# Where four sums of gate and up weights are made: two moved to DMAs that add in SBUF, two to VectorE, none left on GpSimd

## The chip, the cores and the metric

The kernel runs on one core of a Trainium2 chip. TensorE multiplies matrices (PE in the profile; PEld is its load of weights), VectorE (DVE) and ScalarE (ACT) work on elements, GpSimd (POOL) does so more slowly, SyncE (SP) issues DMAs, and 16 DMA engines move data between HBM and SBUF, the memory on the chip. TensorE writes into eight banks of PSUM. The metric is the device time of one execution in microseconds (us); lower is better.

## The reference

Two layers of a model on 512 tokens of width 1024, in float32. A layer has four stages: a gated feed-forward (FFN), a token mixer of three kinds (attention, mLSTM, RWKV), a second FFN, and a per-layer embedding. The change touches the FFN alone, which runs four times:

```python
x = x + 0.5 * rms_norm(swiglu(rms_norm(x, ln_ffn1_pre[l]), w_ffn1_in[l], w_ffn1_out[l]), ln_ffn1_post[l])
# swiglu(h, w_in, w_out): gate, up = halves of h @ w_in (2816 features each);
#                         (silu(gate) * up) @ w_out
```

`w_ffn1_in` is 1024 x 5632: for each of the 2816 features a gate column and an up column.

## The kernel before

Full float32 precision is had by splitting each operand into a high and a low part and adding three products (`mm3`, L160 to L164: high by high, high by low, low by high). `split` (L139 to L141) makes the parts: ScalarE copies the high part (L140), then VectorE, or GpSimd where it is named, subtracts it from the source for the low part (L141). `wsplit` does this for a 128x512 piece of weights, into one of six buffers of the tag "w" (`NW` = 6).

The features go in 22 tiles of 128. A tile m has four 128x512 pieces of weights: g1 and g2 (the gate columns for the first and the second half of the 1024 inputs) and u1 and u2 (the up columns). With the tokens also in two halves, the plain computation would be eight products of pieces by inputs; Winograd's form needs seven, at the price of sums. `turn` (L204 on) makes the sums of the inputs (t1 to t4, lines L233 to L237) for the tokens' second half, and `unit(m, ...)` in `ffn` makes four sums of the weights on GpSimd (L353 to L356): s1 = u1 + u2, s2 = s1 - g1, s3 = g1 - u1, s4 = g2 - s2. The seven products of a tile are, in the order of the program: 1 (g1) and 2 (g2) in `p1` and `p2`, then in `unit` 6 (s2), 7 (s3), 5 (s1), 3 (s4) and 4 (u2), of 12 matmuls each. Between them VectorE combines the results: L362 (after product 6), L365, L367, L369, L370, L373 and last L376, the product of gate and up into the tile h.

What sets the order: there is no order written out by hand in this loop. The program is written unit after unit, and a planner lays the instructions out on each engine's queue by simulated times, in the order of the program where several are ready; on the chip each queue then runs strictly in order, and an instruction whose data are late holds up all that stand behind it. The planner also gives out the buffers. Those that matter here:

- The weights of a tile (`wr`, 128x2048) go into a slot loaded by two DMAs of 512 KB that SyncE issues (`ffn_load`, L311): the first brings g1 and g2, the second u1 and u2. The first four tiles' slots are loaded ahead of the FFN in `ffn_begin`, whose first splits (product 1 of the four tiles) go to GpSimd; for the tiles after them there are three or four slots, so that the load for tile m waits until an earlier tile has had its last split (product 4).
- The sums (`ws`) take the two buffers of the tag "raw", both for one unit: s1 and s2 in one, s3 and s4 in the other.
- The tag "sg" has two buffers, used outside the loop for the scratch of the norms (`junk`, L191) and, in the stage after it (`ffn_out`), for sums of h.
- In PSUM a bank holds the results of two products. Product 3 goes into the other half of product 6's bank, so it waits until L362 has read product 6.

GpSimd also computes the norms' factors (`rms`, L180 and L181) and, at the start of an FFN, one sum and three low parts of the inputs (L237 and L141 on POOL).

Of the kernel before, what the change touches and what calls it, by code (L numbers as in the profile page):

```python
# [21 lines left out]
EPS = 1e-6  # L22
# [51 lines left out]
class Trunk:  # L74
# [50 lines left out]
    def lanes(self, main=MAINL, aux=AUXL, chain=""):  # L125
        """The PSUM tags that the two kinds of tiles go through in turn."""
        self.main, self.aux = cycle(main), cycle(aux)
        self.chain = chain
# [19 lines left out]
    def wblock(self, ap, name, slot=False, raw=None, eng=None):  # L148
        """A block of weights as two halves, each with its high and low parts."""
        c = ap.shape[1]  # L150
        if raw is None:
            raw = self.wraw.tile([128, c], F32, tag="raw", name=name + "_r")
        self.nc.sync.dma_start(out=raw, in_=ap)
        if slot:
            w = self.slot("h", [2, c], name, F32R)
            self.split(w[:, 0], w[:, 1], raw, eng)
            return [(w[:, 0, i * c // 2:(i + 1) * c // 2], w[:, 1, i * c // 2:(i + 1) * c // 2]) for i in range(2)]
        return [self.wsplit(raw[:, i * c // 2:(i + 1) * c // 2], name, eng) for i in range(2)]
# [17 lines left out]
    def rms(self, ss, scale=1.0):  # L176
        """scale / sqrt(mean + EPS) from two halves of the mean square, each over scale squared."""
        g_ = self.nc.gpsimd
        v, r = self.small("v"), self.small("r")
        g_.tensor_scalar(v, ss[0], ss[1], EPS / (scale * scale), op0=ALU.add, op1=ALU.add)  # L180
        g_.tensor_tensor(r, v, self.mhalf, ALU.pow)  # L181
        return r

    def ssq(self, src, name, scale=1.0, dve=False):
        """A half's part of the mean square, over scale squared."""
        junk = self.tmp.tile([128, 512], F32, tag="sg", name="junk")
        s = self.small(name)
        if dve:
            self.nc.vector.tensor_tensor_reduce(junk, src, src, 1.0 / (D * scale * scale), 0.0, ALU.mult, ALU.add, s)
            return s  # L190
        self.nc.scalar.activation(junk, src, AF.Square, scale=D ** -0.5 / scale, accum_out=s)  # L191
        return s
# [12 lines left out]
    def turn(self, t, xn, ffn):  # L205
# [22 lines left out]
        # the sums of Winograd's form of the product by blocks  # L228
# [5 lines left out]
        v_.tensor_tensor(t1, ps[0], t1, ALU.subtract)  # L234
        v_.tensor_tensor(t2, ps[1], t1, ALU.subtract)
        v_.tensor_tensor(t3, ps[1], t3, ALU.subtract)
        g_.tensor_tensor(t4, t4, t2, ALU.subtract)  # L237
# [19 lines left out]
    def out_proj(self, nb, part, blocks, gain, scale, after, tail):  # L257
        """Token-major product of the feature-major parts with weight blocks, post norm, residual."""
# [48 lines left out]
    def ffn_load(self, l, w, ms):  # L307
        rs = [self.slot("h" if m == 3 else "q", [2, 1024], "wr") for m in ms]
        for i in range(2):
            for m, r in zip(ms, rs):  # L310
                self.nc.sync.dma_start(out=r[:, i], in_=self.ins[f"w_ffn{w}_in"][l, m, i])  # L311
        return rs

# [5 lines left out]
    def ffn(self, l, w, after):  # L319
        """The first product goes by Winograd's form of Strassen's seven products: gate and up features by halves of  # L320
        the inputs, halves of the inputs by halves of the tokens."""
# [27 lines left out]
        def unit(m, r, pa, a):  # L349
            g1, g2, u1, u2 = r[:, 0, 0:512], r[:, 0, 512:1024], r[:, 1, 0:512], r[:, 1, 512:1024]  # L350
            ss = [self.wraw.tile([128, 1024], F32, tag="raw", name="ws") for _ in range(2)]
            s1, s2, s3, s4 = (q[:, i * 512:(i + 1) * 512] for q in ss for i in range(2))
            g_.tensor_tensor(s1, u1, u2, ALU.add)  # L353
            g_.tensor_tensor(s2, s1, g1, ALU.subtract)  # L354
            g_.tensor_tensor(s3, g1, u1, ALU.subtract)  # L355
            g_.tensor_tensor(s4, g2, s2, ALU.subtract)  # L356
            pc, pb, pd = self.aux_tile("p63"), self.aux_tile("p75"), self.mm_tile("p4")
            b = self.tmp.tile([128, S], F32, tag="tb1", name="up", bufs=2)
            # an even tile has the tokens' second half first
# [13 lines left out]
            v_.tensor_tensor(b[:, P], pd[:, L], b[:, P], ALU.add)  # L373
            if m % 4 == 0:
                hs.append(self.slot("h", [8, 256], "h"))
            v_.tensor_tensor(hs[m // 4][:, m % 4 * 2:m % 4 * 2 + 2], a.rearrange("p (i t) -> p i t", i=2),  # L376
                             b.rearrange("p (i t) -> p i t", i=2), ALU.mult)
# [10 lines left out]
        for m in range(NM):  # L388
# [4 lines left out]
            unit(m, *q)  # L393
# [3 lines left out]
    def ffn_out(self, hs, blocks, gain, scale, after):  # L397
        """Token-major product of the features with the output weights, by halves of the model's columns. Some of the
        pairs of feature tiles go by Winograd's form of Strassen's products: halves of the tokens by the tiles of the
        pair by halves of the columns."""  # L400
# [5 lines left out]
        # where the halves of a pair's tiles lie, so that the three that products take as they are lie together  # L406
# [149 lines left out]
    def fm_proj(self, ap, name, halves=False):  # L556
        """Feature-major projection of one 128-column tile."""
# [8 lines left out]
    def tm_proj(self, aps, cols, name, eng=None):  # L566
        """Token-major projection; aps hold the rows in k order. Tokens share a bank where they fit."""
# [83 lines left out]
    def weave(self, l):  # L651
        """The chains of the three mixers, their pieces in the order of the plan; a chain that writes its output over
        the projections' inputs lets the last projection go first."""
# [47 lines left out]
    def rwkv_prep(self, l):  # L701
        """RWKV-7 heads in chunks of 64 tokens. A unit is a chunk c of a pair p of heads; its removal-key and key
        rows are stacked on the partitions, the removal-key rows on half (c + p) % 2."""
# [22 lines left out]
        for p in range(2):  # L726
# [9 lines left out]
            # decay and in-context rate  # L736
# [9 lines left out]
            # normalised removal key  # L746
# [18 lines left out]
            # k (1 + (a - 1) k_a)  # L765
# [6 lines left out]
            # bonus  # L772
# [8 lines left out]
    def rwkv_scores(self):  # L781
# [5 lines left out]
        # token-major keys and values; the values are centered over each head, which centers the outputs  # L787
# [18 lines left out]
        # masked scores of [keys, queries] and the part of the solve's right side that values give  # L806
# [33 lines left out]
        # the removal queries token-major  # L840
# [11 lines left out]
    def rwkv_solve(self, q):  # L852
        """The merged inverse for four chunks, applied to the values' part and to the removal queries, which it
        replaces. Yields between tiles."""
# [6 lines left out]
        # a half of a bank's partitions belongs to one half of the rows  # L861
# [17 lines left out]
    def rwkv_scan(self):  # L879
        """The recurrence over the chunks."""  # L880
# [15 lines left out]
        for c in range(8):  # L896
            st, ns = sts[c % 2], sts[(c + 1) % 2]
            tk = slice(c * 64, (c + 1) * 64)
            if c < 7:
                # the diagonal blocks of the pairs' states  # L900
# [45 lines left out]
    def rwkv_norm(self, yt, eng):  # L946
        """Group norm of the centered heads."""
# [13 lines left out]
    def rwkv_back(self, yt, j):  # L961
        """The way back to feature-major, bonus and output gate."""
# [15 lines left out]
    def invert_blocks(self, sm, z, w):  # L978
        """The blocks of 16 of z = (I - M^T)^-1, for the strictly triangular blocks of 64 whose M^T are in sm."""
# [22 lines left out]
    def invert_merge(self, q, sm, z, w):  # L1002
        """Blocks of 16 merged into blocks of 64, for eight units."""
# [31 lines left out]
    def mlstm_proj(self, l):  # L1035
# [4 lines left out]
        # queries and keys through the causal convolution  # L1040
# [27 lines left out]
        # values, gates  # L1068
# [19 lines left out]
        # running maximum  # L1088
# [38 lines left out]
    def mlstm(self, l):  # L1127
        """The chunks of mLSTM, 128 tokens each."""
# [161 lines left out]
    def attention(self, l):  # L1290
# [10 lines left out]
        # high and low parts: the queries' on the halves of the partitions, the keys' on both  # L1301
# [26 lines left out]
        def softmax(t, g):  # L1328
            # the keys of this tile and the last one, the even tile's first
# [188 lines left out]
```

## Time and profile before

| | |
|---|---|
| time, median of 3 runs | 2371.92 us (2371.49 to 2373.13) |
| profiled execution, span from the first to the last instruction | 2369.3 us (the page gives no other time of it) |
| mean granted TensorE clock | 0.977 of full speed |
| busy: TensorE, VectorE, GpSimd, ScalarE | 90%, 85%, 51%, 49% of the span |
| DMA | 208.78 MB, mean 88 GB/s, all issued by SyncE |

In the profile's rows, "ws<-wr" names output and input tiles without their numbers, "128x512" is partitions by elements, "x88" a count; the numbers after the bar are the busy time in all and the mean of one in ns, and after a second bar stands how long the engine was idle just before and what ended that. L140 and L141 are lines of the helper `split`, so one line stands for many places; the tile's name tells them apart ("w<-wr" is a split of g1, g2 or u2, "w<-ws" one of a sum). In rows in order of time the first number is the start and the second the duration, both in us; VectorE's durations overlap a little with the next start, so costs are read from start to start.

### The profile page before, as it was taken

Reading aid. Unit: us, or ns where it says so; the run is one execution under the profiler, and the core shown is the slowest. Engines: PE = TensorE matmul, PEld = TensorE weight load, DVE = VectorE, ACT = ScalarE, POOL = GpSimd, SP = SyncE. Lnnn points to the kernel's source line nnn. Section 1 sums busy time; section 2 is a strip of 40 time slices with the busy share of each in tenths; the row PEclk is TensorE's granted clock in tenths of the full one; section 3 lists DMA queues with packets and bytes.
Section 4 is the critical chain, followed back from the end, with each engine's and each line's share of the span. In section 5 each row is a group of like instructions: output and inputs, shape, how many; then the busy total and the mean of one; then the engine's idle time right before and its main releaser. Section 6 shows DMA issues by size and latency. Waiting matters only on the chain. (4 is left out here: it accounts for less than half of the span.)

```text
span 2369.3 us, 42540 instructions
## 1 busy us (share of the span) xinstructions
PE 2142.1 (90%) x16592; PEld 1975.2 (83%) x16592; DVE 2019.5 (85%) x2990; ACT 1159.0 (49%) x2262; POOL 1215.5 (51%) x1088
## 2 busy tenths in 40 slices
PE   5899988999998899988989989889999989989898
PEld 5888887988778888887878888888887789889787
DVE  8999999645768999998689999986557699999984
ACT  4444544546545444545554445444474454445443
POOL 5665476132236665566365655751332466555751
PEclk8999999999999999999999999999999999999999
DMA  3222222422031222123411221233220312222232
GB/s 151 90 89 90 71 90 90 147 81 55 20 142 54 86 93 90 63 90 116 134 71 72 92 105 55 84 120 122 68 63 7 143 72 90 90 90 75 78 107 80
DMA packets 67513, 208.78 MB, mean 88 GB/s; under 512 B 15728, under 2 KB 16752, under 8 KB 67312
## 3 DMA queue, kind: packets, MB, share of 16 engines
q1 hardware_dynamic: 67312, 206.07, 25.2%
q8 instruction: 130, 2.13, 0.4%
q14 instruction: 71, 0.58, 0.1%
HBM read 199.23 MB, written 6.82 MB: 87 GB/s over the span
## 5 line engine op out<-in xcount | busy, mean ns | idle before, releaser
L162 PE MATMUL p<-xh,w 128*128 128x256 f32 x1408 | 407.8, 291 | 79.8 <-DVE gate L362 77.5
L164 PE MATMUL p<-xh,w 128*128 128x256 f32 x1408 | 401.6, 286 | 13.6 <-DVE w L141 13.6
L163 PE MATMUL p<-xl,w 128*128 128x256 f32 x1408 | 400.8, 285 | 0.1
L141 DVE TENSOR_TENSOR w<-wr,w 128x512 fp32r<-128x512 f32 x249 | 374.8, 1528 | 10.0 <-ACT w L140 9.8
L140 ACT ACTIVATE w<-ws 128x512 fp32r<-128x512 f32 x352 | 210.6, 623 | 305.0 <-POOL ws L354 178.2
L162 PEld LDWEIGHTS p<-xh,w 128*128 128x128 f32 x1408 | 269.9, 192 | 95.5 <-DVE gate L362 89.7
L141 DVE TENSOR_TENSOR w<-ws,w 128x512 fp32r<-128x512 f32 x352 | 327.7, 935 | 3.2 <-ACT w L140 3.1
L162 PE MATMUL p<-tx,w 128*128 128x256 f32 x1056 | 299.9, 285 | 19.1 <-ACT tx L140 14.7
L164 PE MATMUL p<-tx,w 128*128 128x256 f32 x1056 | 298.9, 284 | 5.3 <-DVE w L141 5.2
L163 PE MATMUL p<-tx,w 128*128 128x256 f32 x1056 | 299.2, 284 | 4.7 <-DVE tx L141 4.7
L164 PEld LDWEIGHTS p<-xh,w 128*128 128x128 f32 x1408 | 270.9, 192 | 14.8 <-DVE w L141 14.8
L353 POOL TENSOR_TENSOR ws<-wr 128x512 f32<-128x512 f32 x88 | 119.0, 1352 | 316.2 <-issue 299.5
L163 PEld LDWEIGHTS p<-xl,w 128*128 128x128 f32 x1408 | 270.8, 192 | 0.7 <-DVE xl L141 0.7
L162 PEld LDWEIGHTS p<-tx,w 128*128 128x128 f32 x1056 | 204.7, 194 | 21.2 <-ACT tx L140 15.3
L164 PEld LDWEIGHTS p<-tx,w 128*128 128x128 f32 x1056 | 203.3, 193 | 7.4 <-DVE w L141 7.1
L163 PEld LDWEIGHTS p<-tx,w 128*128 128x128 f32 x1056 | 203.7, 193 | 5.6 <-DVE tx L141 5.6
L466 PE MATMUL y<-wo,hq 128*128 128x256 f32 x1536 | 189.4, 282 | 3.2 <-DVE up L373 2.7
L140 ACT ACTIVATE w<-wr 128x512 fp32r<-128x512 f32 x264 | 163.3, 625 | 57.7 <-PE p L164 41.9
L466 PEld LDWEIGHTS y<-wo,hq 128*128 128x128 f32 x1536 | 184.5, 189 | 4.8 <-DVE up L373 3.5
L355 POOL TENSOR_TENSOR ws<-wr 128x512 f32<-128x512 f32 x88 | 145.9, 1658 | 46.7 <-DVE w L141 45.0
L354 POOL TENSOR_TENSOR ws<-ws,wr 128x512 f32<-128x512 f32 x88 | 147.4, 1675 | 0.6
L356 POOL TENSOR_TENSOR ws<-wr,ws 128x512 f32<-128x512 f32 x88 | 142.4, 1618 | 5.6
(436 smaller groups left out, 5613.4 us busy)
## 6 DMA issues: line engine op xcount, KB each, us to landing
wr<-in_w_ffn_in SPq DMA_DIRECT2D x176, 512.0 KB, 4.1
ws_r<-in_w_ffn_out SPq DMA_DIRECT2D x56, 512.0 KB, 3.2
wo_r<-in_w_ffn_out SPq DMA_DIRECT2D x32, 512.0 KB, 3.3
pkrv_r<-in_w_rw SPq DMA_DIRECT2D x16, 512.0 KB, 3.5
wpg_r<-in_w_ple_gate SPq DMA_DIRECT2D x16, 512.0 KB, 3.4
xd<-x SPq DMA_DIRECT2D x8, 512.0 KB, 2.9
x<-xd SPq DMA_DIRECT2D x8, 512.0 KB, 3.5
pq_r<-in_w_q SPq DMA_DIRECT2D x8, 512.0 KB, 3.5
```

The source lines that it names most:

```text
L140: self.nc.scalar.activation(hi, src, AF.Copy)
L141: (eng or self.nc.vector).tensor_tensor(lo, src, hi.bitcast(F32), ALU.subtract)
L162: mm(out, a[0], b[0], start=first, stop=False)
L163: mm(out, a[0], b[1], start=False, stop=False)
L164: mm(out, a[1], b[0], start=False, stop=last)
L353: g_.tensor_tensor(s1, u1, u2, ALU.add)
L354: g_.tensor_tensor(s2, s1, g1, ALU.subtract)
L355: g_.tensor_tensor(s3, g1, u1, ALU.subtract)
L356: g_.tensor_tensor(s4, g2, s2, ALU.subtract)
L466: nc.tensor.matmul(banks[n][:, u], a[:, x, u * 128:u * 128 + 128], b[y], start=n not in seen, stop=last and i == 2, skip_group_check=True)
```

## The change

The four sums become additions only. Signs are turned where the results are combined: the inputs' sums t1 and t2 change sign, s2 and s4 are now s1 + g1 and g2 + s2, s3 is g1 + u1, product 4's result is subtracted with the operands swapped, and h takes a factor of -1 in a form with a scalar.

s1 is made in place: after a tile's weights are loaded, a DMA issued by GpSimd reads u2 from HBM and adds it to u1 in the slot (`accum_op`). s3 is made in a buffer of its own, of the tag "sg": SyncE loads u1 once more, and a DMA issued by GpSimd adds g1 from HBM. The DMAs for s1 are part of `ffn_load`, so for the first four tiles they are issued in `ffn_begin`; those for s3 come one per unit, in `ffn_sum`. s2 and s4 are computed by VectorE, and take one of the two "raw" buffers per unit instead of both. GpSimd has no sum left in the loop. The number of matmuls is unchanged. Comments that were removed are left out of the diff.

```diff
@@ turn
-        v_.tensor_tensor(t1, ps[0], t1, ALU.subtract)
-        v_.tensor_tensor(t2, ps[1], t1, ALU.subtract)
+        v_.tensor_tensor(t1, t1, ps[0], ALU.subtract)
+        v_.scalar_tensor_tensor(t2, ps[1], -1.0, t1, ALU.mult, ALU.subtract)
         v_.tensor_tensor(t3, ps[1], t3, ALU.subtract)
-        g_.tensor_tensor(t4, t4, t2, ALU.subtract)
+        g_.tensor_tensor(t4, t4, t2, ALU.add)
@@ ffn_load
         for i in range(2):
             for m, r in zip(ms, rs):
                 self.nc.sync.dma_start(out=r[:, i], in_=self.ins[f"w_ffn{w}_in"][l, m, i])
+        for m, r in zip(ms, rs):
+            self.nc.gpsimd.dma_start(out=r[:, 1, 0:512], in_=self.ins[f"w_ffn{w}_in"][l, m, 1][:, 512:1024],
+                                     accum_op=ALU.add)
         return rs
+
+    def ffn_sum(self, l, w, m):
+        s = self.tmp.tile([128, 512], F32, tag="sg", name="gu")
+        w = self.ins[f"w_ffn{w}_in"]
+        self.nc.sync.dma_start(out=s, in_=w[l, m, 1][:, 0:512])
+        self.nc.gpsimd.dma_start(out=s, in_=w[l, m, 0][:, 0:512], accum_op=ALU.add)
+        return s
@@ ffn
-        def unit(m, r, pa, a):
-            g1, g2, u1, u2 = r[:, 0, 0:512], r[:, 0, 512:1024], r[:, 1, 0:512], r[:, 1, 512:1024]
-            ss = [self.wraw.tile([128, 1024], F32, tag="raw", name="ws") for _ in range(2)]
-            s1, s2, s3, s4 = (q[:, i * 512:(i + 1) * 512] for q in ss for i in range(2))
-            g_.tensor_tensor(s1, u1, u2, ALU.add)
-            g_.tensor_tensor(s2, s1, g1, ALU.subtract)
-            g_.tensor_tensor(s3, g1, u1, ALU.subtract)
-            g_.tensor_tensor(s4, g2, s2, ALU.subtract)
+        def unit(m, r, pa, a, s3):
+            g1, g2, s1, u2 = r[:, 0, 0:512], r[:, 0, 512:1024], r[:, 1, 0:512], r[:, 1, 512:1024]
+            ss = self.wraw.tile([128, 1024], F32, tag="raw", name="ws")
+            s2, s4 = ss[:, 0:512], ss[:, 512:1024]
+            v_.tensor_tensor(s2, s1, g1, ALU.add)
+            v_.tensor_tensor(s4, g2, s2, ALU.add)
...
-            v_.tensor_tensor(b[:, P], pd[:, L], b[:, P], ALU.add)
+            v_.tensor_tensor(b[:, P], b[:, P], pd[:, L], ALU.subtract)
...
-            v_.tensor_tensor(hs[m // 4][:, m % 4 * 2:m % 4 * 2 + 2], a.rearrange("p (i t) -> p i t", i=2),
-                             b.rearrange("p (i t) -> p i t", i=2), ALU.mult)
+            v_.scalar_tensor_tensor(hs[m // 4][:, m % 4 * 2:m % 4 * 2 + 2], b.rearrange("p (i t) -> p i t", i=2), -1.0,
+                                    a.rearrange("p (i t) -> p i t", i=2), ALU.mult, ALU.mult)
...
-            unit(m, *q)
+            unit(m, *q, self.ffn_sum(l, w, m))
```

## The prediction

> **What bounds the kernel now.** I read the engine totals first, then the groups of instructions, then the matmuls' waits, and last one unit of the loop over the 22 feature tiles in order of time. The totals and groups on the page:
>
> ```profile
> span 2369.3 us, 42540 instructions
> ...
> PE 2142.1 (90%) x16592; PEld 1975.2 (83%) x16592; DVE 2019.5 (85%) x2990; ACT 1159.0 (49%) x2262; POOL 1215.5 (51%) x1088
> ...
> L162 PE MATMUL p<-xh,w 128*128 128x256 f32 x1408 | 407.8, 291 | 79.8 <-DVE gate L362 77.5
> L164 PE MATMUL p<-xh,w 128*128 128x256 f32 x1408 | 401.6, 286 | 13.6 <-DVE w L141 13.6
> ...
> L141 DVE TENSOR_TENSOR w<-wr,w 128x512 fp32r<-128x512 f32 x249 | 374.8, 1528 | 10.0 <-ACT w L140 9.8
> ...
> L141 DVE TENSOR_TENSOR w<-ws,w 128x512 fp32r<-128x512 f32 x352 | 327.7, 935 | 3.2 <-ACT w L140 3.1
> ...
> L353 POOL TENSOR_TENSOR ws<-wr 128x512 f32<-128x512 f32 x88 | 119.0, 1352 | 316.2 <-issue 299.5
> ...
> L355 POOL TENSOR_TENSOR ws<-wr 128x512 f32<-128x512 f32 x88 | 145.9, 1658 | 46.7 <-DVE w L141 45.0
> L354 POOL TENSOR_TENSOR ws<-ws,wr 128x512 f32<-128x512 f32 x88 | 147.4, 1675 | 0.6
> L356 POOL TENSOR_TENSOR ws<-wr,ws 128x512 f32<-128x512 f32 x88 | 142.4, 1618 | 5.6
> ...
> wr<-in_w_ffn_in SPq DMA_DIRECT2D x176, 512.0 KB, 4.1
> ...
> out<-x SPq DMA_DIRECT2D x8, 256.0 KB, 2.0
> ...
> x<-in_x SPq DMA_DIRECT2D x2, 256.0 KB, 3.2
> ```
>
> TensorE looks like the bound at 90%, but the largest wait of its matmuls is one VectorE instruction, L362, 77.5 us in all. Busy time by stretches, here the 50 us that run through the end of the first per-layer-embedding stage (a stage outside this loop) and the middle of the first unit loop; columns are PE, PEld, DVE, ACT, POOL busy, granted clock, DMA share, GB/s:
>
> ```profile
> 1150.00:1200.00 50.00, 49.21 (x239) 40.73 (x238) 30.77 (x42) 26.90 (x56) 16.55 (x20) 1.00 0.16 53
> 100.00:240.00 140.00, 125.35 (x1035) 122.64 (x1034) 139.59 (x174) 61.15 (x110) 83.70 (x55) 1.00 0.27 98
> ```
>
> In the loop VectorE is busy 139.59 of 140 us and TensorE 125.35: the loop is VectorE's. One unit on VectorE in order of time (start, duration, line, what):
>
> ```profile
> 222.73 0.68 DVE L376 TENSOR_TENSOR h<-gate,up 128x512 f32<-128x512 f32 x1
> 223.33 3.48 DVE L141 TENSOR_TENSOR w<-wr,w 128x512 fp32r<-128x512 f32 x2
> 226.74 0.41 DVE L362 TENSOR_TENSOR gate<-p,gate 128x256 f32<-128x256 f32 x1
> 227.07 1.43 DVE L141 TENSOR_TENSOR w<-wr,w 128x512 fp32r<-128x512 f32 x1
> 228.43 0.41 DVE L367 TENSOR_TENSOR gate<-p,gate 128x256 f32<-128x256 f32 x1
> 228.76 0.68 DVE L141 TENSOR_TENSOR w<-ws,w 128x512 fp32r<-128x512 f32 x1
> 229.36 0.68 DVE L365 TENSOR_TENSOR up<-p,gate 128x512 f32<-128x512 f32 x1
> ...
> 232.28 1.75 DVE L141 TENSOR_TENSOR w<-ws,w 128x512 fp32r<-128x512 f32 x1
> 233.95 0.68 DVE L376 TENSOR_TENSOR h<-gate,up 128x512 f32<-128x512 f32 x1
> ```
>
> From one h (L376) to the next is 11.22 us. The same split (L141) takes 0.68 us at one place and 1.43 to 1.75 at others. The long ones lie where GpSimd runs its sums:
>
> ```profile
> 222.89 1.68 POOL L355 TENSOR_TENSOR ws<-wr 128x512 f32<-128x512 f32 x1 [0.63 <-DVE w L141]
> 224.53 1.74 POOL L354 TENSOR_TENSOR ws<-ws,wr 128x512 f32<-128x512 f32 x1
> 226.34 1.61 POOL L356 TENSOR_TENSOR ws<-wr,ws 128x512 f32<-128x512 f32 x1
> 232.16 1.32 POOL L353 TENSOR_TENSOR ws<-wr 128x512 f32<-128x512 f32 x1 [4.21 <-issue]
> ```
>
> L355, L354 and L356 cover 222.89 to 227.95, where three splits are long; L353 starts at 232.16, where the fourth is. The two engines hold each other up. And TensorE pays for it:
>
> ```profile
> 225.84 0.28 PE L164 MATMUL p<-tx,w 128*128 128x256 f32 x1
> 227.20 0.39 PE L162 MATMUL p<-xh,w 128*128 128x256 f32 x1 [1.08 <-DVE gate L362]
> 227.42 0.28 PE L163 MATMUL p<-xl,w 128*128 128x256 f32 x1
> ```
>
> From L362's own view, who waited for it (us, times):
>
> ```profile
>   PE p L162: 77.5, 66
> ```
>
> L362, queued behind two long splits, frees the bank that product 3 goes into. 66 of the 88 units have this wait, 1.17 us each.
>
> **The change on VectorE.** By start-to-start times, the four long splits take 3.41 + 1.36 + 1.67 = 6.44 us of the 11.22 (3.41 is 226.74 - 223.33, and so on); a short one takes 229.36 - 228.76 = 0.60. With no GpSimd sums in the loop I price all seven at 0.60, so they give back 6.44 - 4 x 0.60 = 4.04. Added are the sums s2 and s4, 128x512 from SBUF, the shape of a split: 2 x 0.60 = 1.20. The product h becomes a form with a scalar, and that form of the same size measures 0.748 at the median against 0.68:
>
> ```profile
> L202 DVE SCALAR_TENSOR_TENSOR xn<-x,r,ln_ffn_pre x32: 740/748/1794, 8.5 to 1907.0; 128x512 f32<-128x512 f32 x32
> ```
>
> so +0.07 (the same form at the stage's start, one per tile of 128 tokens, twice per stage, is +0.07 x 8 in all: nothing). The other sign changes swap operands and cost nothing. VectorE per unit: 11.22 - 4.04 + 1.20 + 0.07 = 8.45 us.
>
> **The change on TensorE.** It has the same 84 matmuls per unit. Around the stall it loses 227.20 - 225.84 = 1.36 instead of the 0.12 of a dense step (227.42 is 0.22 after 227.20, another 0.10), so 1.34 in all, of which the profile books 1.08. A unit without it is 11.22 - 1.34 = 9.88 us. That is above VectorE's 8.45, so TensorE becomes the bound, and the gain stops there. Over the kernel: 77.5 booked + 66 x 0.26 unbooked = 94.7 us. I take 85 of it: an in-order queue that is busy 8.45 of 9.88 will still be late at times, and the first units of each loop get nothing. Lower end 0 (the rivals), upper end 94.7 plus some 10 us for the four starts, where the sums of two units (about 6.3 us each by their means) now stand on GpSimd between the splits that the first products wait for.
>
> **The change on DMA and GpSimd.** Per unit two loads of 512 KB stay; one load of 256 KB (s3's first half) and two adding DMAs of 256 KB, issued by GpSimd, come new. The trace has no adding DMA and no DMA issued by GpSimd. Bounds: not under 2.0 us, the fastest 256 KB row (a store); at most 8.2, twice the 4.1 of a 512 KB load, for reading the destination as well. I take 4.5: the 3.2 us of the 256 KB load plus 1.3 for GpSimd to build it, the price of its cheapest sum. The Trainium skill, "DMA: Bandwidth & Descriptors", section "Anatomy of one DMA — SWDGE (gpsimd) path", fits about 2.0 us plus the bytes over 436 GB/s for DMAs from GpSimd, which would be an estimate of 2.6 us here; it prices copies and not adds, and no row here can test it. By it rival 1 below would not bind and the forecast stands.
>
> Where it is hidden: a tile's weights are loaded when the tile three units before has had its last split, and used two units later; s3's two buffers give the same two units, about 20 us, against 3.2 + 4.5. The 16 engines' share in the loop is 0.27 of 11.22 us, so 3.0 us per unit, for 1 MB; 0.75 MB more at that rate is 2.3, and 5.3 of 9.88 leaves room for adds at twice the price.
>
> At the stage starts, the four adds of the first four tiles queue on GpSimd behind their loads, and in its queue behind them are the first splits and the two small instructions of the post norm. Around the second stage's start:
>
> ```profile
> 711.92 1.85 POOL L356 TENSOR_TENSOR ws<-wr,ws 128x512 f32<-128x512 f32 x1
> 713.73 1.76 POOL L141 TENSOR_TENSOR w<-wr,w 128x512 fp32r<-128x512 f32 x1
> 715.59 0.31 POOL L180 TENSOR_SCALAR v<-ss_post,ss_post 128x1 f32<-128x1 f32 x1
> ```
>
> Today unit 0's sums stand there, and the norm waits until 715.59. Four adds instead, whose issue alone I price at 4 x 1.3 = 5.2, replace four sums of the same price: zero, with +-3 us per start for the loads of the up halves landing late, +-12 over four. If the waits stand ahead of the norms, TensorE's next products are what is late. s3's buffers are shared with the norm's scratch (junk), so s3 of unit 0 is loaded only after the last norm of the inputs; and no product of unit 0 but the first two comes before the products 2 of four tiles, which need tx (ScalarE and TensorE, second start):
>
> ```profile
> 735.13 0.19 ACT L191 ACTIVATION_READ_ACCUMULATOR junk<-x 128x1 f32 x1
> ...
> 749.73 0.58 PE L162 MATMUL p<-tx,w 128*128 128x256 f32 x1 [4.16 <-ACT tx L140]
> ```
>
> 735.3 + 3.2 + 4.5 = 743.0, so 6.7 us of cover.
>
> **Sum.** 2369.3 - 85 + 0 = 2284 of span; the three runs' median, 2371.92, is 2.6 us above the profiled span, so 2287 us. VectorE's order is laid out by a planner, which may put s2 earlier or later; that leads to the rivals.
>
> **Rival 1: the load-and-add chain sets the pace, a little.** The planner issues s2 and s4 of unit m+2 as soon as it thinks they are ready. If it puts them on VectorE just ahead of unit m's last split (product 4), a loop closes: last split of m-1, load, add, s2, s4, last split of m. Its length: 0.1 to the load's issue and 0.5 to the issue of the up half (below: SyncE issues two in 0.80, right after the first of the two splits from 223.33), 4.1 landing, 4.5 add, 3 x 0.60 on VectorE: 11.0 us per unit.
>
> ```profile
> 225.20 0.80 SPq L311 DMA_DIRECT2D wr<-in_w_ffn_in  x2
> ```
>
> Against 11.22 that is 66 x 0.2 = 15 us gained: 2357. For it: the buffers allow exactly this order. Against it: a planner that counts a load and an add as over a unit puts s2 behind the split, the loop then spans two units, and 11.0 is harmless.
>
> **Rival 2, the slower side: the same loop with a dearer add.** With s2 ahead of the last split, the point from which it decides is 11.22 - 6.5 = 4.7 us for one add (6.5 being all the rest of the loop). An add reads and writes its destination; if the moving part of a 256 KB load doubles, and a tiny transfer shows the fixed part,
>
> ```profile
> d<-x SPq DMA_DIRECT2D x16, 16.0 KB, 1.7
> ```
>
> then it is 1.7 + 2 x (3.2 - 1.7) + 1.3 = 6.0, the loop 12.5, and 66 x 1.3 = 86 us come on top: 2458. At the upper bound of 8.2 it would be 14.7 and 2600. Against it: only with that order.
>
> **Rival 3: the adds fill the 16 engines.** Two adds above (9.88 - 3.75)/2, about 3 us of all engines each, where a copy of 256 KB takes 0.75. At 6 us each the unit is 15.8 and the time 2371.9 + 66 x 4.6 = 2675. Nothing in the trace speaks for a factor of eight.
>
> **Rival 4: nothing comes of it.** If TensorE, freed of L362, waits for the next thing at the same pace (the hi parts, half of the splits' wait, on an engine busy 61 of 140 us), the time stays 2372. Against it, L362's 77.5 us are by far the most of its waits in the loop, and the next group (L164 for a split) has 13.6. A clock drop with denser matmuls would do the same, but the 50 us quoted above ran 98% busy at clock 1.00.
>
> **How the numbers follow.** Forecast 0.50 (own range 2265 to 2310), rival 1 0.19, rival 2 0.19, rival 3 0.04, rival 4 0.08. Within 0.2% is about what a measurement here can tell from no change. Faster: nearly all of the forecast, most of rival 1: 0.64. Same: rival 4 and a little of rival 1: 0.09. Slower: rivals 2 and 3 and the rest of 1: 0.27. The range, 2265 to 2430, leaves out half of rival 2, rival 3, and a twentieth below.
>
> **What would show it.** Right: no long splits in the loop (L141 near 0.68 us for both groups), the wait on L362 nearly gone, unit period near 9.9 us, TensorE at 95% or more there and VectorE at about 85%. Rivals 1 and 2: s2 on VectorE with idle time ahead of it that an adding DMA ends, and a period of 11 to 12.5. Rival 3: DMA share near 1 in the loop. The forecast is wrong if the splits stay long without GpSimd's sums, or if GpSimd's queue, blocked on loads, delays the norms at the four starts by more than 3 us each.

## The result, and the profile after

The changed kernel takes 2315.17 us (median of 4 runs, 2309.84 to 2323.17); the kernel before took 2371.70 (4 runs, 2369.83 to 2373.13). The ratio is 0.9766, with a 95% interval of 0.9745 to 0.9786. The profiled execution is the fastest of the four, at 2309.84 us. Faster, then, but by 56.5 us where the forecast had 85.

The page of the changed kernel, engine totals, groups and DMA landings (the last number of a landing row is the median time from issue to landing, in us):

```profile
span 2308.1 us, 42939 instructions
...
PE 2135.2 (93%) x16592; PEld 1976.0 (86%) x16592; DVE 1815.7 (79%) x3166; ACT 1167.5 (51%) x2261; POOL 816.7 (35%) x912
...
q0 software_dynamic: 25344, 46.15, 12.5%
...
L162 PE MATMUL p<-xh,w 128*128 128x256 f32 x1408 | 404.9, 289 | 28.4 <-DVE gate L372 23.3
...
L141 DVE TENSOR_TENSOR w<-wr,w 128x512 fp32r<-128x512 f32 x337 | 234.4, 696 | 10.0 <-ACT w L140 9.9
...
L365 DVE TENSOR_TENSOR ws<-wr 128x512 f32<-128x512 f32 x88 | 61.6, 701 | 133.2 <-issue 130.3
...
wr<-in_w_ffn_in SPq DMA_DIRECT2D x176, 512.0 KB, 6.2
...
wr<-in_w_ffn_in POOLq DMA_DIRECT2D x88, 256.0 KB, 4.4
gu<-in_w_ffn_in POOLq DMA_DIRECT2D x88, 256.0 KB, 5.7
```

The long splits are gone: the group of splits of loaded weights has a mean of 696 ns, where it had 1528. (The group is larger, x337, because s1 now lies in the slot of the loaded weights.) The wait of product 3 on the combination behind product 6, which was L362 and is L372 now, fell from 77.5 to 23.3 us. A new wait has come: 130.3 us ahead of L365, which is s2 on VectorE. The profile gives it to "issue", that is, it names no engine; L365 reads what the adding DMA wrote, and below it starts when that DMA has landed. The loads of 512 KB land in 6.2 us instead of 4.1.

The same 140 us of the first loop as in the prediction (columns PE, PEld, DVE, ACT, POOL busy, granted clock, DMA share, GB/s), after:

```profile
100.00:240.00 140.00, 134.57 (x1118) 132.25 (x1117) 110.42 (x210) 67.66 (x119) 23.39 (x27) 1.00 0.69 172
```

VectorE is no longer full: 110.42 of 140 us. But TensorE isn't full either, at 134.57. The new wait of VectorE's, from its view of waits (us in all, times, longest):

```profile
DVE ws L365 <- issue: 130.3, 55, 5.8
```

One of the long cases, on VectorE in order of time:

```profile
160.57 0.68 DVE L387 SCALAR_TENSOR_TENSOR h<-up,gate 128x512 f32<-128x512 f32 x1
161.17 0.69 DVE L141 TENSOR_TENSOR w<-wr,w 128x512 fp32r<-128x512 f32 x1
163.94 0.69 DVE L365 TENSOR_TENSOR ws<-wr 128x512 f32<-128x512 f32 x1 [2.09 <-issue]
...
171.15 0.68 DVE L387 SCALAR_TENSOR_TENSOR h<-up,gate 128x512 f32<-128x512 f32 x1
175.59 0.69 DVE L365 TENSOR_TENSOR ws<-wr 128x512 f32<-128x512 f32 x1 [3.76 <-issue]
176.19 0.68 DVE L141 TENSOR_TENSOR w<-wr,w 128x512 fp32r<-128x512 f32 x1
```

and the DMAs issued meanwhile, from SyncE's queue and from GpSimd:

```profile
161.88 0.81 SPq L311 DMA_DIRECT2D wr<-in_w_ffn_in  x2
...
176.91 0.80 SPq L311 DMA_DIRECT2D wr<-in_w_ffn_in  x2
```

```profile
171.45 0.86 POOL L314 DMA_DIRECT2D wr<-in_w_ffn_in  x1 [8.70 <-DVE w L141]
```

This add's landing, in us after its issue (least, median, most; it is one DMA):

```profile
DMA to landing us min/median/max: 4.1/4.1/4.1
```

After the first h the order is h, the last split of the unit (161.17), s2 (163.94). After the second it is h, s2 (175.59), the last split (176.19). In that second order a chain closes. The last split at 161.17 frees a slot; the two loads are issued at 161.88; the add, which needs the second of them, is issued at 171.45 and lands 4.1 us later, at 175.5; s2 runs at 175.59 and only then the next last split, which frees the slot for the loads at 176.91. From one pair of loads to the next that is 15.0 us. This is rival 1 of the prediction, in every third unit: VectorE's queue has s2 ahead of the last split there, and directly behind it in the other two (where s2 waits too, 2.09 us at 163.94). The periods, from one combination behind product 6 to the next, are about 9.8, 10.5 and 12.6 us in turn.

The profile puts the wait of the add at 171.45 down to a split (DVE w L141). But for each of the 18 tiles that are loaded inside this loop the add is issued 0.55 us after the second load has landed, so it is the load that it waits for. Why the add came so late is seen in the landings of the loads. The pair issued at 161.88:

```profile
DMA to landing us min/median/max: 6.9/7.8/8.6
```

and the pair issued at 176.91:

```profile
DMA to landing us min/median/max: 3.3/3.8/4.2
```

The first pair was issued together with the add for s3 of another unit (L323 at 161.89 in GpSimd's queue), the second 4.7 us after such an add. Of the nine pairs from 143.8 to 228.09 us, the three issued 4.0 to 4.7 us after such an add took 3.2 to 4.4 us, and the six issued within 0.8 us of one took 5.7 to 8.6. That is not the whole of it: earlier in the same loop the pairs issued at 100.17 and 121.03, 0.3 and 0.9 us before such an add, took only 3.2 to 4.8.

Where the 61.2 us of the two spans (2369.3 and 2308.1) come from can be counted in the trace, by the starts of the combination behind product 6 (L362 before, L372 after), 22 in each of the four loops:

| us, four loops together | before | after |
|---|---|---|
| first start to last start | 928.3 | 861.0 |
| of that the first 7 periods | 295.1 | 264.6 |
| of that the last 14 periods | 633.2 | 596.4 |
| all the rest of the span | 1441.0 | 1447.1 |

The loops gave 67.3 us, and the rest took 6.1 back. Nearly half of the gain, 30.5 us, is in the first seven periods.

### The profile page after: what moved, and what is told of

Its sections match the earlier page's. It is cut to its first block, busy times and chain, and to the rows that moved or that the text cites. A ratio compares the mean times of both kernels' runs of the same rounds, so it can differ in the third digit from the quotient of the medians.

```text
span 2308.1 us, 42939 instructions
## 1 busy us (share of the span) xinstructions
PE 2135.2 (93%) x16592; PEld 1976.0 (86%) x16592; DVE 1815.7 (79%) x3166; ACT 1167.5 (51%) x2261; POOL 816.7 (35%) x912
## 3 DMA queue, kind: packets, MB, share of 16 engines
q0 software_dynamic: 25344, 46.15, 12.5%
## 5 line engine op out<-in xcount | busy, mean ns | idle before, releaser
L162 PE MATMUL p<-xh,w 128*128 128x256 f32 x1408 | 404.9, 289 | 28.4 <-DVE gate L372 23.3
L140 ACT ACTIVATE w<-wr 128x512 fp32r<-128x512 f32 x352 | 219.9, 628 | 227.5 <-PE p L164 211.7
L314 POOL DMA_DIRECT2D wr<-in_w_ffn_in x88 | 77.8, 895 | 499.5 <-DVE up L380 156.3
L141 DVE TENSOR_TENSOR w<-wr,w 128x512 fp32r<-128x512 f32 x337 | 234.4, 696 | 10.0 <-ACT w L140 9.9
L164 PEld LDWEIGHTS p<-tx,w 128*128 128x128 f32 x1056 | 201.7, 191 | 12.9 <-DVE w L141 12.6
L365 DVE TENSOR_TENSOR ws<-wr 128x512 f32<-128x512 f32 x88 | 61.6, 701 | 133.2 <-issue 130.3
L477 PE MATMUL y<-wt,xh 128*128 128x256 f32 x768 | 125.4, 301 | 26.6 <-DVE xh L141 15.1
L140 ACT ACTIVATE w<-ws 128x512 fp32r<-128x512 f32 x176 | 110.0, 625 | 69.6 <-PE p L164 69.2
L477 PEld LDWEIGHTS y<-wt,xh 128*128 128x128 f32 x768 | 107.5, 202 | 36.4 <-DVE xh L141 19.0
L323 POOL DMA_DIRECT2D gu<-in_w_ffn_in x88 | 79.8, 907 | 164.0 <-DVE w L141 38.8
```

What stands on the lines that cost most here:

```text
L140: self.nc.scalar.activation(hi, src, AF.Copy)
L141: (eng or self.nc.vector).tensor_tensor(lo, src, hi.bitcast(F32), ALU.subtract)
L162: mm(out, a[0], b[0], start=first, stop=False)
L164: mm(out, a[1], b[0], start=False, stop=last)
L314: self.nc.gpsimd.dma_start(out=r[:, 1, 0:512], in_=self.ins[f"w_ffn{w}_in"][l, m, 1][:, 512:1024], accum_op=ALU.add)
L323: self.nc.gpsimd.dma_start(out=s, in_=w[l, m, 0][:, 0:512], accum_op=ALU.add)
```

## The experiments

Each is the changed kernel with one thing changed, the last two with two. The first four ran side by side (the kernel before there: 2370.45 us, 7 runs), the next four (2371.21) and the last three (2369.99) likewise, each with 4 runs. Ratios are to the kernel before.

**s2 later.** All DMAs stay; s2 and s4 are held in VectorE's queue behind the split of s1 (product 5) of the unit before, some 8 us later, most of a unit, than the place where they closed the chain.

```diff
+            if m >= 2:                          # lasts[m - 1]: the split of s1 of unit m-1
+                with tc.issue_after(lasts[m - 1]):
+                    v_.tensor_tensor(s2, s1, g1, ALU.add)
+                    v_.tensor_tensor(s4, g2, s2, ALU.add)
```

> The changed kernel with one thing more: VectorE's two sums s2 and s4 of a unit are held, in the order of VectorE's queue, behind the split of s1 (product 5) of the unit before; nothing else is moved by hand, and all DMAs and adds stay. Theory A (the chain: last split of a tile, load into its slot, add, s2; where the planner puts s2 ahead of the next last split, the chain closes after one unit, and the later units of a loop take about 11.0 us on average instead of 9.9): with s2 later the chain spans two units and binds no more, VectorE's idle time ahead of s2 (130 us in the changed kernel) falls below 30, the period goes to 9.9 to 10.1, time 2283 to 2297. Rival B (the order does not matter; the units are long because the 16 DMA engines are at a share of 0.6 to 0.7 and data come late whatever waits for them, or because TensorE can't go faster): same as the changed kernel, 2308 to 2320.

Measured: 2255.11 us (2248.19 to 2258.0), ratio 0.9509 (0.9491 to 0.9527), 60 us below the changed kernel, and 28 us below the range that theory A gave. From its page, the product behind which the wait was, and the landings; then the 140 us:

```profile
L162 PE MATMUL p<-xh,w 128*128 128x256 f32 x1408 | 398.3, 284 | 3.9 <-ACT xh L140 1.8
...
wr<-in_w_ffn_in SPq DMA_DIRECT2D x176, 512.0 KB, 6.5
...
wr<-in_w_ffn_in POOLq DMA_DIRECT2D x88, 256.0 KB, 4.1
gu<-in_w_ffn_in POOLq DMA_DIRECT2D x88, 256.0 KB, 6.4
```

```profile
100.00:240.00 140.00, 140.00 (x1191) 140.00 (x1191) 124.84 (x229) 74.58 (x131) 25.56 (x30) 1.00 0.69 176
```

TensorE is busy in all of the 140 us. The loads and adds land no sooner than in the changed kernel (6.5, 4.1, 6.4 against 6.2, 4.4, 5.7), and the DMA share is the same 0.69: only the place of two instructions in a queue has moved. So the chain is the cause, and not traffic that slows TensorE. Theory A had the right cause but took from the prediction what the loop gives without the chain, which was too little; the next three expectations share this, and their runs came out 13 to 46 us below the ranges that they gave. The last 14 periods are 9.88 to 9.89 us each in all four loops.

The starts of the combination behind product 6 within the first loop, before, after and with s2 later (the count and the first and last start stand in each row, in us):

```profile
L362 DVE TENSOR_TENSOR gate<-p,gate x15: 410/411/412, 102.7 to 260.4; 128x256 f32<-128x256 f32 x15
```

```profile
L372 DVE TENSOR_TENSOR gate<-p,gate x15: 409/416/418, 102.8 to 252.7; 128x256 f32<-128x256 f32 x15
```

```profile
L378 DVE TENSOR_TENSOR gate<-p,gate x16: 409/418/419, 102.6 to 250.9; 128x256 f32<-128x256 f32 x16
```

Over 14, 14 and 15 periods: 157.7 / 14 = 11.26, 149.9 / 14 = 10.71, 148.3 / 15 = 9.89.

**The up half first.** Inside the loop the up half, which the add needs, is loaded ahead of the gate half. The order of the engines' work stays.

```diff
-        for i in range(2):
+        for i in (0, 1) if len(rs) > 1 else (1, 0):
```

> The changed kernel with the two loads of a tile swapped inside the loop: the half with u1 and u2 is issued first, so the add can start earlier; the order on VectorE, TensorE and ScalarE is the same as in the changed kernel. Theory A: the chain is shorter by the 0.5 us of one issue and by part of the transfer that now comes behind, 1 to 3 us in all; the idle time ahead of s2 falls from 130 to 50 to 90 us, time 2292 to 2306. Rival B: bytes and share are the same, so 2308 to 2320.

Measured: 2259.06 us (2256.14 to 2263.43), ratio 0.9532 (0.9517 to 0.9546). The wait ahead of s2:

```profile
DVE ws L365 <- issue: 34.5, 21, 2.4
```

The order that closes the chain is still there: splits, sums and combinations follow each other on VectorE exactly as in the changed kernel, in all four loops. But the chain is shorter by one load, and that does nearly as much as moving s2. The wait falls from 130.3 us in 55 to 34.5 in 21, where 50 to 90 us were expected.

**All four sums on VectorE**, with no adding DMA and no second load.

```diff
+            v_.tensor_tensor(s3, g1, s1, ALU.add)    # s1 is still u1 here
+            v_.tensor_tensor(s1, s1, u2, ALU.add)
             v_.tensor_tensor(s2, s1, g1, ALU.add)
```

> All four sums on VectorE: s3 into its own buffer, s1 in place in the slot, s2 and s4 as in the change; no adding DMA, no second load, nothing on GpSimd in the loop. VectorE per unit 8.45 + 2 x 0.60 = 9.65 us, just under TensorE's 9.88. Theory A: no chain with an add, so period 9.9 to 10.2 and 2285 to 2305; about as e8. Rival B: if the load of the DMA engines was what made the units long, this one alone of the two gets down to 2285, and e8 does not.

Measured: 2271.56 us (2269.23 to 2274.28), ratio 0.9584 (0.9568 to 0.96). The 140 us:

```profile
100.00:240.00 140.00, 140.00 (x1191) 140.00 (x1190) 137.21 (x262) 74.38 (x130) 1.84 (x2) 1.00 0.28 103
```

TensorE is full here too, at a DMA share of 0.28 instead of 0.69, and the last 14 periods are 9.86 to 9.91 us: the DMAs are worth nothing in the loop. What this kernel loses against s2 later lies outside the loops, 1476.0 us against 1448.6; its loops are 14.6 us shorter (793.1 against 807.7).

**Plain copies.** GpSimd's DMAs copy and do not add. This leaves out two sums: s1 holds u2 alone, s3 holds g1 alone.

```diff
-            self.nc.gpsimd.dma_start(out=r[:, 1, 0:512], in_=..., accum_op=ALU.add)
+            self.nc.gpsimd.dma_start(out=r[:, 1, 0:512], in_=...)
```

> The changed kernel with the two DMAs of GpSimd as plain copies instead of adds, so that s1 becomes u2 and s3 becomes g1 and the result is another; order on all compute engines as in the changed kernel. It prices the add: a copy of 256 KB issued by GpSimd should land in 2.5 to 3.5 us where the add takes 4.4 (for s1) and 5.7 (for s3) at the median, and the share of the engines that GpSimd's queue takes should fall from 12.5% to 5 to 7%. Theory A: the chain is 1 to 2 us shorter, the idle time ahead of s2 60 to 100 us, time 2295 to 2308. Rival B (share of the engines): also faster, by about half of the loss, 2295 to 2305; this run does not tell A from B but sizes the term.

Measured: 2249.17 us (2247.59 to 2252.6), ratio 0.949 (0.9476 to 0.9504). GpSimd's queue and the landings:

```profile
q0 software_dynamic: 14080, 46.15, 6.0%
...
wr<-in_w_ffn_in SPq DMA_DIRECT2D x176, 512.0 KB, 4.5
...
wr<-in_w_ffn_in POOLq DMA_DIRECT2D x88, 256.0 KB, 3.2
gu<-in_w_ffn_in POOLq DMA_DIRECT2D x88, 256.0 KB, 2.9
```

The same 46.15 MB take 6.0% of the 16 engines' span as copies and 12.5% as adds; a copy lands 1.2 us (3.2 against 4.4) and 2.8 us (2.9 against 5.7) sooner. The 512 KB loads land in 4.5 us beside copies, and in 6.2 beside adds: the adds lengthen the chain twice, by themselves and through the loads. VectorE's order is again exactly that of the changed kernel, so the chain is still closed in every third unit, and it costs nothing at this length.

**s2 without the add.** s2 is made as u2 + g1, so it does not read what the add writes; its value is another. All DMAs stay.

```diff
-            v_.tensor_tensor(s2, s1, g1, ALU.add)
+            v_.tensor_tensor(s2, u2, g1, ALU.add)
```

> Part of the computation is changed: s2 is made as u2 + g1, so it no longer reads what the adding DMA writes; all DMAs, adds and the order of the program stay. Theory (the add of s1 is a link of the chain): without its 4.4 us and its issue, s2 waits for the two loads alone, which land 6 to 8 us after the last split; the long units of 12.5 us go, the period is 9.9 to 10.1, the wait ahead of the first sum is under 25 us in all, and the time is 2250 to 2268. Rival (the loads, made late by the adds' traffic, are enough to close the chain): every third unit stays long, period 10.4 and more, 2285 to 2315.

Measured: 2247.10 us (2245.16 to 2248.51), ratio 0.948 (0.9463 to 0.9497); last 14 periods 9.89 to 9.92 us. With every load and every add in place and as slow as before (6.4, 4.1 and 6.3 us), taking the add out of what s2 waits for removes the whole loss, and no wait is left ahead of s2. On VectorE s2 still stands ahead of the last split in every third unit of the last three loops, and more often in the first. The load alone, then, does not make the chain bind.

**Two units of room.** s2 and s4 of every unit stand directly behind the last split of the unit two before, so never ahead of it.

```diff
+            if m >= 2:                          # lasts[m - 2]: the last split of unit m-2
+                with tc.issue_after(lasts[m - 2]):
+                    sums()                      # s2 and s4
```

> All DMAs as in the changed kernel; s2 and s4 of every unit are held directly behind the last split of the unit two before, so none stands ahead of it as every third did. Theory (the chain counts by the number of units it spans): from the last split of unit m-3 to s2 of unit m the load and the add take some 12.6 us as in the long units of the changed kernel, from there to the last split of unit m-1 VectorE needs about 8 us: 20.6 us for two units, 10.3 each against 9.88. The wait ahead of s2 stands in nearly every unit (over 80 us in all, over 50 times), the period is 10.1 to 10.5 us, the time 2255 + 60 x 0.4 = 2279, range 2264 to 2295. Rival (a chain over two units is harmless, as the prediction had it): period 9.9 us, 2248 to 2260.

Measured: 2289.11 us (2284.89 to 2296.35), ratio 0.9657 (0.9636 to 0.9679); last 14 periods 10.03, 10.16, 10.29 and 10.32 us in the four loops. The wait:

```profile
DVE ws L366 <- issue: 91.0, 45, 3.0
```

So a chain over two units, which the prediction called harmless, costs 34 us against s2 later: s2 has about one unit after the slot is freed, and load and add take more than that. By this comparison, of the 60 us that the changed kernel loses, s2 ahead of the split in every third unit makes some 26 (2315.17 - 2289.11), and s2 directly behind it is enough for the other 34.

**s1 and s3 on GpSimd.** No adding DMA and no second load; GpSimd makes two sums and VectorE the other two.

```diff
+            g_.tensor_tensor(s3, g1, s1, ALU.add)
+            g_.tensor_tensor(s1, s1, u2, ALU.add)
             v_.tensor_tensor(s2, s1, g1, ALU.add)
```

> No adding DMA and no second load: s1 and s3 are made by GpSimd, s2 and s4 by VectorE. Theory (GpSimd's sums hold up VectorE's splits): the four sums of the kernel before lengthened VectorE by 4.04 us per unit, so two cost about 2.0, and VectorE needs 8.45 + 2.0 = 10.5 us per unit, more than TensorE's 9.88. The splits that lie beside the two sums take 1.4 us and more, the period in the loop's last 14 units is 10.2 to 10.8 us, and the time is 2255 (the run with s2 later) plus some 80 units x 0.6 = 2300, range 2280 to 2325. Rival (the splits of the kernel before were long for another reason, the number of loads or the place in the queue): splits 0.68 us, period 9.9 us, 2248 to 2265.

Measured: 2287.76 us (2285.58 to 2292.4), ratio 0.9651 (0.9637 to 0.9666). Its groups, then the 140 us:

```profile
L359 POOL TENSOR_TENSOR gu<-wr 128x512 f32<-128x512 f32 x88 | 129.2, 1468 | 512.6 <-DVE w L141 306.7
L141 DVE TENSOR_TENSOR w<-wr,w 128x512 fp32r<-128x512 f32 x337 | 289.4, 860 | 9.5 <-ACT w L140 9.5
...
L141 DVE TENSOR_TENSOR w<-ws,w 128x512 fp32r<-128x512 f32 x176 | 179.3, 1019 | 0.2 <-ACT w L140 0.2
...
L360 POOL TENSOR_TENSOR wr<-wr 128x512 f32<-128x512 f32 x88 | 143.2, 1628 | 6.2
```

```profile
100.00:240.00 140.00, 138.14 (x1160) 137.06 (x1159) 139.62 (x229) 71.08 (x126) 43.18 (x28) 1.00 0.27 100
```

The splits are long again, 860 and 1019 ns in the mean, so it is GpSimd's sums that hold them up. The size was missed: VectorE is full (139.62 of 140), but of the last 14 periods the first twelve are 9.98 us in the mean (the last two are 8.9, with no next tile's products between), so two sums cost it about 9.98 - 8.45 = 1.5 us and not 2.0, and VectorE ends up level with TensorE. The period of 10.2 to 10.8 us did not come. The loss stands at the beginnings of the loops and outside them instead: the first seven periods of the four loops take 268.9 us against 254.0 with s2 later, and the time outside the loops is 1465.3 against 1448.6. The Trainium skill, "SBUF — State Buffer", section "Who interferes with whom", says that a VectorE instruction with two inputs from SBUF contends with a GpSimd instruction that reads SBUF, and one with at most one such input, outside the modes that use two ports, does not. The traces agree: in the same 140 us the splits, with two SBUF inputs, take 0.68 us where no sum of GpSimd runs beside them and 1.3 to 1.4 where one does throughout. And in the prediction's lines of the kernel before, L362, which has one input from PSUM, keeps its 0.41 us at 226.74, in the midst of L356 (226.34, 1.61 us), where the split behind it takes 1.43.

**s1 on VectorE**, s3 still by an adding DMA.

```diff
+            v_.tensor_tensor(s1, s1, u2, ALU.add)
             v_.tensor_tensor(s2, s1, g1, ALU.add)
```

> s1 is made by VectorE in place, s2 and s4 too; only s3 stays an adding DMA. Theory (the chain runs through the load, the add for s1 and s2): without the add the chain is load, s1, s2, s4, some 6 to 8 us after the last split, under 9.88; VectorE needs 8.45 + 0.6 = 9.05 us per unit. The period of the last 14 units is 9.9 us, the idle time ahead of the sums on VectorE is under 20 us in all, and the time is 2250 to 2272. Rival (any adding DMA in the loop delays it, s3's too): period 10.3 us and more, 2285 to 2315, with TensorE waiting for the adding DMA of s3.

Measured: 2252.93 us (2250.33 to 2254.14), ratio 0.95 (0.9486 to 0.9514); last 14 periods 9.69 to 9.84 us. VectorE does wait, for the loads instead of the add:

```profile
DVE wr L362 <- DMA wr<-in_w_ffn_in: 57.4, 49, 3.6
```

That is more than the 20 us expected, but TensorE does not see it, and the time came where the theory had it. An adding DMA whose result is not on the way to the next slot (s3's) is harmless here.

**Adds for the first four tiles only**, VectorE from the fifth on.

```diff
-        for m, r in zip(ms, rs):
+        for m, r in zip(ms, rs) if len(rs) > 1 else ():
             self.nc.gpsimd.dma_start(..., accum_op=ALU.add)
...
+            if m >= G:
+                v_.tensor_tensor(s3, g1, s1, ALU.add)
+                v_.tensor_tensor(s1, s1, u2, ALU.add)
```

> Only the first four tiles of each FFN have adding DMAs; from the fifth tile on all four sums are on VectorE, with neither an add nor a second load. Theory (the adds are worth something only at the four starts, where all sums on VectorE cost some 20 us net; in the loop TensorE's 9.88 us bind either way): period 9.9 us in the last 14 units, the time outside the loops 1448 us as in the changed kernel, the loops 800 to 808, so 2248 to 2258, as with s2 later. Rival (VectorE, at about 9.65 of 9.88 us per unit with two more sums, is late often): period 10.0 to 10.2, 2262 to 2275.

Measured: 2272.37 us (2270.05 to 2276.53), ratio 0.9586 (0.957 to 0.9602). The periods are 9.89 to 9.93 us, as the theory had it, but the time is the rival's. The loss is outside the loops, 1462.8 us against 1448.6. Against the run with s2 later, the output stages after the four loops end 1.7 to 2.3 us later after the last combination behind product 6, and the way from there to the last loop (the second FFN of layer 2) is another 6 us longer. So the adds at the four starts were not what the kernel with all sums on VectorE lacked. Two more sums per unit leave VectorE (134.94 of 140 us busy here) a backlog at the end of the loop; that it is the whole of the loss is an argument and was not tested alone.

**Both cures, and s1 on VectorE with s2 later.** The up half first and s2 later together; and s1, s2, s4 on VectorE behind the split of s1 of the unit before.

> The two cures of the chain together: the up half is loaded first inside the loop, and s2 and s4 stand behind the split of s1 of the unit before. If the chain is all that the changed kernel lost, there is nothing left for the second cure: period 9.9 us, 2248 to 2258, as with s2 later alone. Rival (waits on late loads remain with s2 later alone, under other names): 5 us and more faster than it, 2240 to 2248.

> s1, s2 and s4 on VectorE, held behind the split of s1 of the unit before; only s3 stays an adding DMA. Against the run with s1 on VectorE (2252.93 us, where VectorE waited 57.4 us for loads ahead of s1): if these waits lay beside TensorE's work, 2248 to 2258 again; if they cost a part of their 57.4 us, 2235 to 2247.

Measured: 2257.57 us (2256.22 to 2257.77), ratio 0.9522 (0.9507 to 0.9537), and 2257.49 us (2256.71 to 2258.14), ratio 0.9524 (0.9507 to 0.9541). Neither gains anything on one cure alone. The loop is at TensorE's pace in all of them, and what is left between 2247 and 2258 us lies outside the loops (1442 to 1456 us) more than in them (799 to 808), where the instructions' order differs a little from kernel to kernel; its causes were not traced.

The fastest kernels that compute the reference are those with s1 on VectorE (2252.93) and with s2 later (2255.11), which can't be told apart; the two kernels just above are 2 to 5 us behind. The first two are 2.6 to 2.7% below the changed kernel.

## Why the prediction was right, and where it was wrong

**What bounds the kernel before: right.** Without GpSimd's sums the splits fell to 0.70 us in the mean, and two of the sums put back brought long splits back. VectorE between the two h of the timeline above takes 171.15 - 160.57 = 10.58 us, of which the profile books 2.1 as waits: 8.4 to 8.5, where the prediction had 8.45.

**TensorE's floor of 9.88 us: right.** The period that was worked out from one stall in the trace of before is what seven of the kernels show when the chain is gone (9.80 to 9.93 us over the last 14 periods of each loop).

**The gain that this makes possible: mis-sized, too small.** The step that failed is "the first units of each loop get nothing", and with it the upper end of 94.7. With s2 later the loops give 928.3 - 807.7 = 120.6 us. The last 14 periods of four loops give 56 x (11.31 - 9.88) = 80, and the first seven another 295.1 - 254.0 = 41.1. Products 1 and 2 of the first four tiles are made ahead of the loop, so TensorE has five products for each of those units, 9.88 x 5 / 7 = 7.06 us, and one period of 7.07 does stand there in each of the last three loops of that run. VectorE had its whole work to do in them (in the first loop before, it was busy 72.54 of the 73.90 us of the first seven periods), so its relief counts for more there, and not for nothing.

**What the in-order queue loses: mis-sized, far too small.** The forecast gave up 10 of 94.7 us for it. In the changed kernel it is 861.0 - 807.7 = 53.3 us, 42.7 of them in the last 14 periods (596.4 against 553.7). That is rival 1's chain, which the forecast held to be absent and the rival held to be in every unit at 11.0 us. It closes in every third unit, and binds over two units in others. The errors, 26 us too little gain (120.6 against 94.7), 43 us too little loss (53.3 against 10) and the starts' 6 us, make 24 us of span (2308.1 against 2284); the other 4 us of the 28 between 2287 and 2315 are that the profiled execution was the fastest of its four, 5 us below their median. The time lies outside the forecast's own range (2265 to 2310), between the forecast and rival 1 (2357), and within the whole range because the chain had been given a price of its own as a rival. That it came as near to the forecast as 28 us is in part luck: two errors, of 26 and of 43 us, went opposite ways.

**The chain's length: the load was the wrong term, the add was not.** Rival 1 had 0.6 to the issue, 4.1 for the load, 4.5 for the add and 1.8 on VectorE: 11.0 us. The timeline above has 0.7 to the issue, 9.6 until the add is issued (the pair of loads, landing up to 8.6 us after its issue), 4.1 from there to s2, and 0.6 to the split: 15.0. The price of the add holds (4.5 against a median of 4.4; 5.7 for s3's). The load's does not: its landing was taken from a trace without adds, and beside them it goes from 4.1 to 6.2 us at the median and to 8.6 where a pair collides with an add. Rival 2 saw a chain of 12.5 us, with the dearer link at the wrong place; it did not come to 2458 us because the chain closes in every third unit only.

**"A planner that puts s2 behind the split ... the loop then spans two units, and 11.0 is harmless": wrong at the chain's real length.** Two units of room cost 34 us.

**The add's price by a page: too low.** The estimate of 2.6 us from the Trainium skill, "DMA: Bandwidth & Descriptors", section "Anatomy of one DMA — SWDGE (gpsimd) path", is for copies; copies of this size from GpSimd landed in 2.9 and 3.2 us here, and adds in 4.4 and 5.7. By that estimate rival 1 would not have bound, and it did; but with the loads of the timeline above the chain would have been 15.0 - 4.1 + 2.6 = 13.5 us, so the larger error was the load.

**DMA engines, starts, clock.** The share of the 16 engines in the loop is 0.69, where 5.3 of 9.88 us, 0.54, was worked out, since an add takes 2.1 times a copy; there is still room, as the run with s2 later shows at the same share. The starts were priced at 0 with 12 either way. All that lies outside the loops took 6.1 us, and it stands at the starts: TensorE's waits of over 1.5 us there for the normed inputs and for tx, at the second to the fourth FFN, grew from 18.2 to 24.4 us, by 1.4, 3.8 and 1.0. So one start passes the 3 us that the prediction named as a sign of being wrong, and the others do not; what made the waits longer was not traced. The granted clock in the 140 us is 1.00 as before.

## What to carry to other kernels

When work goes from an engine to a DMA, follow the buffer round: what frees it, the load, the add, the first reader, and where that reader stands in its engine's queue against the instruction that frees the buffer. A chain like this costs nothing or 60 us of 2300 by the place of one instruction, with the same work and traffic; give the reader more room than the chain's length under the new traffic, not under the old. And where some units of a loop have less to do on the engine that will bind, relief on the other engine can be worth more there.

## What the hardware showed that was not expected

A DMA from GpSimd that adds 256 KB into SBUF takes 2.1 times the engine time of a copy (12.5% against 6.0% of the span for 46.15 MB, in 25344 packets against 14080), lands 1.2 to 2.8 us later, and slows the 512 KB loads beside it: 6.2 us at the median beside adds, 4.5 beside copies, and among nine pairs of one loop 5.7 to 8.6 us with an add issued within 0.8 us against 3.2 to 4.4 with none, though earlier pairs of that loop do not all fit. TensorE, at a DMA share of 0.69, keeps the pace that it has at 0.28. And the changed kernel varies more from run to run, 0.6% (2309.84 to 2323.17), than the kernel before, 0.1%; the chain is not shown to be the reason, since the kernel with s2 later varies by 0.4% (2248.19 to 2258.0).
